# Two of four weight sums by accumulating DMA in the FFN, one pool of 4 KB tiles, and a deeper pipeline

## The chip, the cores and the metric

The kernel runs on one core of a Trainium2 chip, at batch 1 with 512 tokens. The engines that matter are TensorE (PE in the profile; its weight loads stand apart as PEld), VectorE (DVE), ScalarE (ACT), GpSimd (POOL) and SyncE (SP). DVE, ACT and POOL do elementwise work. SP and POOL also issue the DMAs: plain loads go through SP, and loads that add onto what already lies in the destination tile (accumulate DMAs) go through POOL. Each engine works through its instructions in a fixed order, and waits on semaphores for what others must have done first.

The metric is the device time of one execution in microseconds (us). Besides the time of each run there is one profiled execution with its trace.

## The reference, cut to what matters

```python
D_MODEL = 1024; SEQ = 512; DEPTH = 2; CHUNK = 128; RET_HEADS = 4; FFN_HIDDEN = 2816

def sgu_mixer(h, w_in, w_s, b_s, ln_g, ln_b, w_out):
    u, v = jnp.split(jax.nn.gelu(h @ w_in), 2, axis=-1)
    v = layernorm(v, ln_g, ln_b)                   # then in chunks of 128 tokens, 8 groups
    mixed = jnp.einsum('gts,bcsgd->bctgd', tril(w_s), v) + b_s
    return (u * mixed) @ w_out

def retention(h, positions, w_in, gn_g, w_out):
    q, k, v, g = split(h @ w_in)                   # 4 heads; q and k 256 wide, v and g 512 wide
    q, k = rotary(q, positions), rotary(k, positions) * 256 ** -0.5
    o = chunkwise_recurrence(q, k, v)              # decayed causal scores in chunks, state between
    o = rms(o) * gn_g
    return (o * jax.nn.silu(g)) @ w_out

def swiglu(h, w_gu, w_down):
    a, b = jnp.split(h @ w_gu, 2, axis=-1)         # each 2816 wide
    return (jax.nn.silu(a) * b) @ w_down

def reference(x, ...):
    h = x
    h = h + sgu_mixer(rmsnorm(h)); h = h + swiglu(rmsnorm(h))     # layer 0
    h = h + retention(rmsnorm(h)); h = h + swiglu(rmsnorm(h))     # layer 1
    return rmsnorm(h, final_norm_g)
```

All is float32.

## The kernel before, in words

**Precision.** Each operand of a large product is split into two halves of type float32r: ACT copies the high half (`wh`, L187) and DVE subtracts to get the low half (`wl`, L188). `three` then issues three matmuls for each product of tiles: high by high (L209), high by low (L210), low by high (L211).

**Seven products in place of eight.** Most large weight matrices go through `seven`, which multiplies two-by-two blocks with seven products, in the order P1, P7, P6, Q4, P5, P2, P3. Four of the seven need a sum of weight blocks: P7 (a tile `t`), P6 and Q4 (which add two more blocks to the same `t`), and P5 (`b12` with `b11`). The left factors, sums of blocks of the activations, come from `combos` (names with `h_P7h`, `z_P6l` and so on; `xA` does it for the FFN's input, `xP_f`). A product is cut into two groups of two 128-row tiles of weight; one group of one product is a *job*, so one call of `seven` has 14 jobs.

**Where the weight sums are made.** With `dma_sums=True` (the FFN's down projections `dn`, the retention's `vg` and `ro0`) the sums of P7 and P5 are made by the load itself: SP loads one block, then POOL issues an accumulate DMA of the other block onto the same tile (`onto`, L292), which must wait for the first. The sums of P6 and Q4 are made by DVE (`add`, L315). In the FFN's gate-and-up units, `gu`, all four sums are made by DVE.

**The FFN.** One FFN runs `gl` (the leftover 256 columns of each half), then units `gu_0`, `gu_1`, `dn_0`, `gu_2`, `gu_3`, `dn_1`, `gu_4`, then `dn_2`. The `gu` units are `turned`: their matmuls are 128x256, and 336 of them make one unit. A `dn` unit has 168 matmuls of 128x512 and adds into the residual `X`. `last_rows` does the rest of a layer's last product (`so`, `ro1`, `dn_2`), token chunk by token chunk, so that the next norm can begin early: the normed rows are transposed and split into `XH` (ACT, L591) and `XL` (DVE, L592), on which the next layer's first matmuls wait.

**Layer 0's mixer** projects `v0`, `v1`, `u0`, `u1`, normalizes `v` (L765), mixes over tokens (L794), and gates `u` (L782 to L785). **Layer 1's mixer** runs for each head `qk`, `vg`, the scores and the values; then `ro0` (a `seven`) and `ro1`.

**Rotary tables.** The sine and cosine for the retention are worked out on DVE (L825 to L862) in small steps that are put between the jobs of layer 0's FFN (`extra`, `more`).

**What sets the order.** `pipeline` walks over the jobs. Before job number `done` runs, the loads of all jobs below `done + FETCH` (6) have been issued, and the splits of all jobs below `done + PREP` (3):

```python
while f < len(weighted) and f < done + FETCH:
    jobs[weighted[f]].fetch()
...
while p < len(weighted) and p < done + PREP:
    jobs[weighted[p]].prep()
```

A scheduler places the instructions of each engine in an order that starts from this one. Weight tiles come from the pool `gen` of 21 tiles of 4 KB per partition; raw activations and left factors of `last_rows` come from `raws`, 8 tiles of 8 KB; `XH` and `XL` are one fixed buffer each.

Of the kernel before, what the change touches and what calls it, by code (L numbers as in the profile page):

```python
# [25 lines left out]
PREP = 3  # L26
FETCH = 6
N_GEN = 21
N_RAW = 8
N_TMP = 5  # L30
EPS = 1e-6
# [18 lines left out]
class Job:  # L50


    def __init__(self, fetch=None, prep=None, run=None):
        self.fetch, self.prep, self.run = fetch, prep, run


def pipeline(jobs):
    n = len(jobs)
    weighted = [i for i, j in enumerate(jobs) if j.prep is not None]
    f = p = 0  # L60
    done = 0
    for i, job in enumerate(jobs):
        while f < len(weighted) and f < done + FETCH:
            jobs[weighted[f]].fetch()
            f += 1
        while p < len(weighted) and p < done + PREP:
            jobs[weighted[p]].prep()
            p += 1
        if job.prep is not None:
            done += 1  # L70
        job.run()
# [3 lines left out]
def trunk(ctx, tc, x, positions, mix_g, ffn_g, fin_g, sgu_w_in, sgu_w_s, sgu_b_s, sgu_ln_g, sgu_ln_b,  # L75
# [5 lines left out]
    raws = ctx.enter_context(tc.tile_pool(name="raws", bufs=N_RAW))  # L81
# [10 lines left out]
    def RAW(name, dtype=F32, shape=(P, 4, T)):  # L92
        return raws.tile(list(shape), dtype, tag="r", name=name)
# [11 lines left out]

    def captured(*fns):

        n = len(jobs)
        for fn in fns:
            fn()  # L110
        new = jobs[n:]
        del jobs[n:]
        units = []
        for j in new:
            if j.prep is not None or not units:
                units.append([j])
            else:
                units[-1].append(j)
        return units

    def merged(a, b):

        i = j = 0
        while i < len(a) or j < len(b):
            if j == len(b) or (i < len(a) and i * len(b) <= j * len(a)):
                jobs.extend(a[i])
                i += 1
            else:
                jobs.extend(b[j])
                j += 1  # L130
# [143 lines left out]

    def seven(name, w, r0, np_, c1, c2, A, evac, mid=None, dma_sums=False, turned=False):

# [3 lines left out]
        steps = [(s, min(2, np_ - s)) for s in range(0, np_, 2)]  # L280
# [4 lines left out]
        def load(key, i, j, s, nk):  # L285
            raw[key, s] = fetch_tile(f"{name}_{key}_{s}", w, r0 + i * np_ + s, nk, ((c1, T) if j == 0 else (c2, T),))

        def onto(key, i, j, s, nk):
            c0 = c1 if j == 0 else c2
            k0 = r0 + i * np_ + s  # L290
            src = w[k0 * P:(k0 + nk) * P, c0:c0 + T].rearrange("(a p) n -> p a n", p=P)
            nc.gpsimd.dma_start(raw[key, s][:, 0:nk, :], src, accum_op=ALU.add)  # L292

        def fetch(p, s, nk):
            if p == "P1":
                load("b11", 0, 0, s, nk)
            elif p == "P7" and dma_sums:
                load("t", 1, 1, s, nk)
                onto("t", 0, 1, s, nk)
            elif p == "P5" and dma_sums:  # L300
                load("b12", 0, 1, s, nk)
                onto("b12", 0, 0, s, nk)
            elif p == "P7":
                load("b12", 0, 1, s, nk)
                load("t", 1, 1, s, nk)
            elif p == "Q4":
                load("b21", 1, 0, s, nk)
            elif p == "P2":
                load("b21", 1, 0, s, nk)
            elif p == "P3":  # L310
                load("b22", 1, 1, s, nk)

        def add(dst, other, s, nk):
            d, o = raw[dst, s][:, 0:nk, :], raw[other, s][:, 0:nk, :]
            nc.vector.tensor_tensor(d, d, o, ALU.add)  # L315

        def prep(p, s, nk):
            use = {"P1": "b11", "P7": "t", "P6": "t", "Q4": "t", "P5": "b12", "P2": "b21", "P3": "b22"}[p]
            extra = {"P7": "b12", "P6": "b11", "Q4": "b21", "P5": "b11"}.get(p)
            if extra and not (dma_sums and p in ("P7", "P5")):  # L320
                add(use, extra, s, nk)
            parts[p, s] = split(raw[use, s], f"{name}_{p}_{s}", nk)

        chain = {"P1": "X", "P7": "Y", "P6": "X", "Q4": "Y", "P5": "X", "P2": "Z", "P3": "X"}
# [802 lines left out]
```

## Time and profile before

| quantity | value |
|---|---|
| median of 3 runs | 1269.76 us (1268.45 to 1273.49) |
| profiled execution, its own time | 1267.79 us |
| span of its trace | 1266.1 us |
| instructions in the trace | 18063 |
| PE busy | 1220.4 us, 96% of the span |
| DVE busy | 947.4 us, 75% |
| ACT busy | 616.8 us, 49% |
| POOL busy | 47.4 us, 4% |
| DMA moved | 183.91 MB, mean 145 GB/s |

A row of the list of waits reads: engine, the line that waited, the instruction and line it waited for, then the microseconds in total, how often, and the longest. A row of windows gives a stretch of the trace, its length, the busy time of each engine in it, then the clock granted to PE as a share of full speed, the busy share of the 16 DMA engines and what they moved. In the timeline a row is one instruction with its start and its duration, and in brackets the idle time just before it. A matmul's duration reaches past the start of the next one, since matmuls are pipelined, so the distance between two starts is the cost of one. In the list of DMAs, SPq and POOLq are the queues of SP and POOL, and the last number is the median time from issue to landing.

### The profile page before, as it was taken

Reading aid. Unit: us, or ns where it says so; the run is one execution under the profiler, and the core shown is the slowest. Engines: PE = TensorE matmul, PEld = TensorE weight load, DVE = VectorE, ACT = ScalarE, POOL = GpSimd, SP = SyncE. Lnnn points to the kernel's source line nnn. Section 1 sums busy time; section 2 is a strip of 40 time slices with the busy share of each in tenths; the row PEclk is TensorE's granted clock in tenths of the full one; section 3 lists DMA queues with packets and bytes.
Section 4 is the critical chain, followed back from the end, with each engine's and each line's share of the span. In section 5 each row is a group of like instructions: output and inputs, shape, how many; then the busy total and the mean of one; then the engine's idle time right before and its main releaser. Section 6 shows DMA issues by size and latency. Waiting matters only on the chain. (4 is left out here: it accounts for less than half of the span.)

```text
span 1266.1 us, 18063 instructions
## 1 busy us (share of the span) xinstructions
PE 1220.4 (96%) x7290; PEld 1081.8 (85%) x7290; DVE 947.4 (75%) x1080; ACT 616.8 (49%) x772; POOL 47.4 (4%) x49
## 2 busy tenths in 40 slices
PE   8999999998999999999999999889999999999997
PEld 7787889987999798978878878668899989997995
DVE  4467489999779884786766757697488799878864
ACT  4424255544544463656455564465355445544452
POOL 0000000000001000000000000000000010000000
PEclk9999999999999999999999999899999999999999
DMA  7224225457636763356445645466215476556531
GB/s 266 85 83 128 64 84 156 137 146 228 183 117 164 219 198 94 84 156 169 127 140 125 185 123 150 110 178 211 84 44 174 142 175 196 170 158 187 189 116 67
DMA packets 101987, 183.91 MB, mean 145 GB/s; under 512 B 6376, under 2 KB 19728, under 8 KB 101904
## 3 DMA queue, kind: packets, MB, share of 16 engines
q1 hardware_dynamic: 91984, 163.86, 40.8%
q0 software_dynamic: 9920, 18.90, 9.1%
q8 instruction: 57, 0.93, 0.3%
q14 instruction: 26, 0.21, 0.1%
HBM read 180.64 MB, written 2.10 MB: 144 GB/s over the span
## 5 line engine op out<-in xcount | busy, mean ns | idle before, releaser
L211 PE MATMUL X_gu<-xP_f,wl_gu_P 128*128 128x256 f32 x480 | 135.8, 283 | 0.0
L210 PE MATMUL X_gu<-xP_f,wh_gu_P 128*128 128x256 f32 x480 | 135.8, 283 | 0.0
L209 PE MATMUL X_gu<-xP_f,wh_gu_P 128*128 128x256 f32 x480 | 135.8, 283 | 0.0
L188 DVE TENSOR_TENSOR wl_gu_P<-wr_gu_b,wh_gu_P 128x1024 fp32r<-128x1024 f32 x80 | 95.0, 1219 | 29.6 <-ACT wh_gu_P L187 29.6
L210 PEld LDWEIGHTS X_gu<-xP_f,wh_gu_P 128*128 128x128 f32 x480 | 92.1, 192 | 0.2
L209 PEld LDWEIGHTS X_gu<-xP_f,wh_gu_P 128*128 128x128 f32 x480 | 92.1, 192 | 0.2
L211 PEld LDWEIGHTS X_gu<-xP_f,wl_gu_P 128*128 128x128 f32 x480 | 92.1, 192 | 0.0
L187 ACT ACTIVATE wh_gu_P<-wr_gu_b 128x1024 fp32r<-128x1024 f32 x80 | 79.5, 1052 | 18.4 <-DVE wl_gu_P L188 5.0
L315 DVE TENSOR_TENSOR wr_gu_t<-wr_gu_t,wr_gu_b 128x1024 f32<-128x1024 f32 x60 | 71.7, 1217 | 2.1 <-DMA wr_gu_t<-in_ffn_w_gu 2.0
L187 ACT ACTIVATE wh_gu_P<-wr_gu_t 128x1024 fp32r<-128x1024 f32 x40 | 41.6, 1057 | 50.3 <-DVE wr_gu_t L315 40.6
L188 DVE TENSOR_TENSOR wl_vg_P<-wr_vg_b,wh_vg_P 128x1024 fp32r<-128x1024 f32 x32 | 38.6, 1219 | 26.8 <-ACT wh_vg_P L187 26.8
L209 PE MATMUL ps_qk<-XH,wh_qk 128*128 128x512 f32 (+1 forms) x160 | 56.1, 352 | 1.4 <-ACT xr_r L622 0.8
L211 PE MATMUL ps_qk<-XH,wl_qk 128*128 128x512 f32 (+1 forms) x160 | 55.6, 348 | 0.0
L210 PE MATMUL ps_qk<-XL,wh_qk 128*128 128x512 f32 (+1 forms) x160 | 55.4, 347 | 0.0
L188 DVE TENSOR_TENSOR wl_gu_P<-wr_gu_t,wh_gu_P 128x1024 fp32r<-128x1024 f32 x40 | 48.0, 1218 | 7.1 <-ACT wh_gu_P L187 7.1
L209 PE MATMUL Y_gu<-xP_f,wh_gu_P 128*128 128x256 f32 x160 | 45.3, 283 | 0.0
L210 PE MATMUL Y_gu<-xP_f,wh_gu_P 128*128 128x256 f32 x160 | 45.3, 283 | 0.0
L211 PE MATMUL Y_gu<-xP_f,wl_gu_P 128*128 128x256 f32 x160 | 45.3, 283 | 0.0
L209 PE MATMUL Y_gu<-XH,wh_gu_Q 128*128 128x256 f32 x160 | 45.3, 283 | 0.0
L210 PE MATMUL Y_gu<-XL,wh_gu_Q 128*128 128x256 f32 x160 | 45.3, 283 | 0.0
L211 PE MATMUL Y_gu<-XH,wl_gu_Q 128*128 128x256 f32 x160 | 45.3, 283 | 0.0
L209 PE MATMUL Z_gu<-XH,wh_gu_P 128*128 128x256 f32 x160 | 45.3, 283 | 0.0
(507 smaller groups left out, 3872.9 us busy)
## 6 DMA issues: line engine op xcount, KB each, us to landing
wr_gu_b<-in_ffn_w_gu SPq DMA_DIRECT2D x100, 512.0 KB, 4.0
wr_dn_b<-in_ffn_w_down SPq DMA_DIRECT2D x40, 512.0 KB, 4.6
wr_vg_b<-in_ret_w_in SPq DMA_DIRECT2D x40, 512.0 KB, 3.7
wr_gu_t<-in_ffn_w_gu SPq DMA_DIRECT2D x20, 512.0 KB, 5.2
wr_qk<-in_ret_w_in SPq DMA_DIRECT2D x32, 256.0 KB, 3.1
wr_dn<-in_ffn_w_down SPq DMA_DIRECT2D x12, 512.0 KB, 4.0
wr_ro_b<-in_ret_w_out SPq DMA_DIRECT2D x10, 512.0 KB, 4.1
wr_u<-in_sgu_w_in SPq DMA_DIRECT2D x8, 512.0 KB, 4.1
```

The source lines that it names most:

```text
L187: nc.scalar.activation(h, s, AF.Copy)
L188: nc.vector.tensor_tensor(l, s, f32(h), ALU.subtract)
L209: nc.tensor.matmul(o, ah, bh, start=start, stop=False, skip_group_check=True)
L210: nc.tensor.matmul(o, ah, bl, start=False, stop=False, skip_group_check=True)
L211: nc.tensor.matmul(o, al, bh, start=False, stop=stop, skip_group_check=True)
L315: nc.vector.tensor_tensor(d, d, o, ALU.add)
```

## The change

**Constants.** `PREP` goes from 3 to 5 and `FETCH` from 6 to 8. A job whose load is an accumulate (`early`) is fetched 12 jobs ahead (`EARLY`), past the jobs between.

**Pools.** `raws` goes away, and `gen` grows from 21 to 38 tiles of 4 KB. What was held in 8 KB tiles is now held in halves (`xr`, `hq`, `zq`, `yq`, the pairs of `xA`, the left factors of `last_rows`). `XH` and `XL` come from a pool of two buffers and are new tiles for every norm.

**Sums.** In the ten `gu` units the sums of P7 and P5 are made by accumulate DMAs too, as in `dn`, `vg` and `ro0`: four accumulates of 512 KB for each unit, forty in all, in place of forty additions on DVE. The number of plain loads of a unit stays at 12 of 512 KB, since `b12` is now loaded for P5 where it had been loaded for P7.

**Left factors.** P1, P7 and P6 of a `dn` unit are asked for during the last three products of the `gu` unit before it, those of `ro0` during the last head's `vg`, and those of `last_rows` during `ro0` and `gu_4`.

**Last product.** In `seven`, only the last two groups of P3 wait for each other; with two groups this is what was there before.

**Rotary tables.** Their steps move out of layer 0's FFN and stand between the jobs of `u0` and `u1` in layer 0's mixer (`turn_tables`).

```diff
-PREP = 3
-FETCH = 6
-N_GEN = 21
-N_RAW = 8
+PREP = 5
+FETCH = 8
+EARLY = 12
+ASK = 3
+N_GEN = 38
+SUMS_X = ("P7", "P5")
+SUMS_GU = ("P7", "P5")
...
 def pipeline(jobs):
...
+    for job in jobs:
+        while e < n and e < done + EARLY:
+            if weighted[e].early:
+                weighted[e].fetch()
+            e += 1
+        while f < n and f < done + FETCH:
+            if not weighted[f].early:
+                weighted[f].fetch()
             f += 1
+        while p < n and p < done + PREP:
+            weighted[p].prep()
             p += 1
...
-    raws = ctx.enter_context(tc.tile_pool(name="raws", bufs=N_RAW))
+    xp = ctx.enter_context(tc.tile_pool(name="xp", bufs=2))
...
+        def fetch(p, g, s, nk):
+            def load(key, i, j):
+                raw[key, g, s] = G(f"wr_{name}_{key}_{g}_{s}")
+                nc.sync.dma_start(raw[key, g, s][:, 0:nk, :], source(i, j, g, s, nk))
+
+            def onto(key, i, j):
+                nc.gpsimd.dma_start(raw[key, g, s][:, 0:nk, :], source(i, j, g, s, nk), accum_op=ALU.add)
+
+            if p == "P7":
+                load("t", 1, 1)
+                (onto if p in dma_sums else load)("t" if p in dma_sums else "o", 0, 1)
+            elif p == "P1":
+                load("b11", 0, 0)
+            elif p == "Q4":
+                load("b21", 1, 0)
+            elif p == "P2":
+                load("b21", 1, 0)
+            elif p == "P5":
+                load("b12", 0, 1)
+                (onto if p in dma_sums else load)("b12" if p in dma_sums else "o", 0, 0)
...
+            jobs.append(Job(lambda p=p, st_=st_: fetch(p, *st_), lambda p=p, st_=st_: prep(p, *st_), lambda i=i: run(i),
+                            early=p in dma_sums))
...
-    project_t("u0", w_in, ((0, T),), after_u0, mix0_col)
-    project_t("u1", w_in, ((T, T),), after_u1, mix0_col)
+    project_t("u0", w_in, ((0, T),), after_u0, mix0_col, mid={kp: turn_tables for kp in range(4)})
+    project_t("u1", w_in, ((T, T),), after_u1, mix0_col, mid={kp: turn_tables for kp in range(4)})
...
-            seven(f"gu{l}_{i}", w, 0, 4, i * T, FF + i * T, xparts, evac, mid, turned=True)
+            seven(f"gu{l}_{u}", w, rows(0, KD), u * T, FF + u * T, xparts, evac, mid, dma_sums=SUMS_GU, turned=True)
...
-        unit(1, {"P5": lambda: A[0]("P1"), "P2": lambda: A[0]("P7")})
+        unit(1, {("Q4", 1): lambda: A[0]("P1", 0), ("P5", 0): lambda: A[0]("P7", 0), ("P2", 1): lambda: A[0]("P6", 0)})
         down(0)
...
-        second({"P2": lambda: outA("P1")} if hd == 3 else None)
+        second({("P6", 1): lambda: outA("P1", 0), ("P2", 0): lambda: outA("P7", 0), ("P2", 1): lambda: outA("P6", 0)} if hd == 3 else None)
```

Three places of the new order are needed later on. A row is the line, the kind of instruction and the names of what it writes and reads, with the shape.

**DVE where layer 0's FFN begins.** `XL` is the low half of the normed input, for which `gl`'s matmuls wait; `wl_gu_0_P` are the low halves of `gu_0`'s first weights; L315 are weight sums. Before:

```order
L603 SCALAR_TENSOR_TENSOR xs_f_0_1302<-X,nf_so_1295,g_f_1145 128x1024
L188 TENSOR_TENSOR wl_gl_3_1335<-wr_gl_3_1099,wh_gl_3_1334 128x1024
L592 TENSOR_TENSOR XL<-xT_f_1_1338,XH 128x8x128
L188 TENSOR_TENSOR wl_gu_0_P_0_1380<-wr_gu_0_b_0_1112,wh_gu_0_P_0_1379 128x1024
L315 TENSOR_TENSOR wr_gu_0_t_1332<-wr_gu_0_t_1332,wr_gu_0_b_0_1330 128x1024
L188 TENSOR_TENSOR wl_gu_0_P_2_1408<-wr_gu_0_b_2_1124,wh_gu_0_P_2_1407 128x1024
L315 TENSOR_TENSOR wr_gu_0_b_0_1330<-wr_gu_0_b_0_1330,wr_gu_0_b_0_1112 128x1024
L315 TENSOR_TENSOR wr_gu_0_t_1377<-wr_gu_0_t_1377,wr_gu_0_b_2_1375 128x1024
L188 TENSOR_TENSOR wl_gu_0_P_0_1450<-wr_gu_0_t_1332,wh_gu_0_P_0_1449 128x1024
L656 TENSOR_TENSOR xS_f_1477<-xr_f_0_1213,xr_f_1_1214 128x1024
L592 TENSOR_TENSOR XL<-xT_f_0_1411,XH 128x8x128
```

Now:

```order
L595 SCALAR_TENSOR_TENSOR xs_f_0_1414<-X,nf_so_1407,g_f_1255 128x1024
L170 TENSOR_TENSOR wl_gu_0_P_0_2_1446<-wr_gu_0_b_0_2_1214,wh_gu_0_P_0_2_1445 128x1024
L584 TENSOR_TENSOR XL_f_1322<-xT_f_1_1449,XH_f_1321 128x8x128
L170 TENSOR_TENSOR wl_gu_0_P_0_0_1492<-wr_gu_0_t_0_1144,wh_gu_0_P_0_0_1491 128x1024
L584 TENSOR_TENSOR XL_f_1322<-xT_f_0_1525,XH_f_1321 128x8x128
L302 TENSOR_TENSOR wr_gu_0_t_0_1144<-wr_gu_0_t_0_1144,wr_gu_0_b_0_0_1202 128x1024
```

Between the last two `XL` there stood seven instructions, three of them weight sums; now there stands one.

**SP where the FFN goes from `gu_3` to `dn_1` (layer 0).** Rows are loads of weight tiles. `t` and `b12` of `dn_1` are the tiles onto which POOL then accumulates. Before:

```order
L179 DMA wr_gu0_3_b21_0_3423<-in_ffn_w_gu 128x2x512
L179 DMA wr_gu0_3_b21_2_3464<-in_ffn_w_gu 128x2x512
L179 DMA wr_gu0_3_b22_0_3495<-in_ffn_w_gu 128x2x512
L179 DMA wr_gu0_3_b22_2_3528<-in_ffn_w_gu 128x2x512
L179 DMA wr_dn0_1_b11_0_3558<-in_ffn_w_down 128x2x512
L179 DMA wr_dn0_1_b11_2_3594<-in_ffn_w_down 128x2x512
L179 DMA wr_dn0_1_t_0_3625<-in_ffn_w_down 128x2x512
L179 DMA wr_dn0_1_t_2_3664<-in_ffn_w_down 128x2x512
```

Now:

```order
L277 DMA wr_gu0_3_b21_0_0_3409<-in_ffn_w_gu 128x2x512
L277 DMA wr_gu0_3_b21_0_2_3444<-in_ffn_w_gu 128x2x512
L277 DMA wr_dn0_1_t_0_0_3474<-in_ffn_w_down 128x2x512
L277 DMA wr_gu0_3_b22_0_0_3477<-in_ffn_w_gu 128x2x512
L277 DMA wr_dn0_1_t_0_2_3509<-in_ffn_w_down 128x2x512
L277 DMA wr_gu0_3_b22_0_2_3512<-in_ffn_w_gu 128x2x512
L277 DMA wr_dn0_1_b11_0_0_3542<-in_ffn_w_down 128x2x512
L277 DMA wr_dn0_1_b11_0_2_3578<-in_ffn_w_down 128x2x512
```

`t` of `dn_1` moved from behind `dn_1`'s own first loads to ahead of `gu_3`'s last.

**DVE in layer 0's mixer, ahead of the normalization of `v`.** `turns`, `turn`, `frac` and `sum` are the rotary tables' steps; `ry_ln` is the end of the chain for the variance; `v_0` and `v_1` are what is normalized. Before:

```order
L526 SCALAR_TENSOR_TENSOR ru_ln_564<-rt_ln_562,ra_ln 128x4
L528 SCALAR_TENSOR_TENSOR ry_ln_566<-ru_ln_564,ry_ln_560 128x4
L765 TENSOR_SCALAR v_0_324<-v_0_324,mv,ry_ln_566 128x512 x2
L765 TENSOR_SCALAR v_0_329<-v_0_329,mv,ry_ln_566 128x512 x2
L765 TENSOR_SCALAR v_1_529<-v_1_529,mv,ry_ln_566 128x512 x2
```

Now:

```order
L735 TENSOR_TENSOR frac_763<-turns_761,turn_764 128x512
L518 SCALAR_TENSOR_TENSOR ry_ln_576<-ru_ln_574,ry_ln_570 128x4
L757 TENSOR_TENSOR sum_767<-turns,frac_763 128x512
L514 TENSOR_TENSOR rt_ln_578<-ry_ln_576 128x4
L734 CAST turn_769<-sum_767 128x512
L516 SCALAR_TENSOR_TENSOR ru_ln_580<-rt_ln_578,ra_ln 128x4
L735 TENSOR_TENSOR turns<-sum_767,turn_769 128x512
L518 SCALAR_TENSOR_TENSOR ry_ln_582<-ru_ln_580,ry_ln_576 128x4
L811 TENSOR_SCALAR v_0_324<-v_0_324,mv,ry_ln_582 128x512 x2
```

The steps of the tables now alternate with the chain of `ry_ln`; eighteen of them, from the one that writes `ahl` on, stand ahead of the normalization, where there was none.

503 lines of the change are left out of this document (231 added, 272 removed).

## The prediction

> **What bounds the kernel now.** I read the page first, then the waits of PE, then windows of 30 us to see where those waits lie, then the timeline at the longest.
>
> ```profile
> span 1266.1 us, 18063 instructions
> PE 1220.4 (96%) x7290; PEld 1081.8 (85%) x7290; DVE 947.4 (75%) x1080; ACT 616.8 (49%) x772; POOL 47.4 (4%) x49
> q1 hardware_dynamic: 91984, 163.86, 40.8%
> q0 software_dynamic: 9920, 18.90, 9.1%
> ```
>
> PE is the bound, with 45.7 us of its span idle. The change does not take matmuls away, so its gain can only come from PE's idle time and from time in which PE ran at a lower clock. The longest waits:
>
> ```profile
> PE ps_gl L210 <- DVE XL L592: 5.2, 4, 2.5
> PE X_ro L209 <- ACT wh_ro_P L187: 4.4, 2, 2.7
> PE X_dn L209 <- ACT wh_dn_P L187: 3.5, 3, 1.7
> PE Y_dn L209 <- ACT wh_dn_Q L187: 3.2, 4, 2.6
> PE Z_vg L210 <- DVE wl_vg_P L188: 2.0, 3, 1.0
> PE X_vg L210 <- DVE wl_vg_P L188: 1.8, 1, 1.8
> PE X_ro L210 <- DVE wl_ro_P L188: 1.7, 2, 0.9
> PE pv L209 <- ACT vh L1012: 1.6, 2, 0.8
> PE Y_ro L209 <- ACT wh_ro_Q L187: 1.1, 1, 1.1
> PE Y_dn L209 <- ACT wh_dn_P L187: 1.1, 1, 1.1
> ```
>
> They add up to 25.6 us in 23 waits. No row is of a `gu` unit: they are of `gl`, `dn`, `vg` and `ro0`. The windows agree (the columns are the stretch, its length, PE, PEld, DVE, ACT, POOL, clock, DMA share, GB/s):
>
> ```profile
> 0.00:30.00 30.00, 25.55 (x111) 21.32 (x112) 15.42 (x33) 13.65 (x20) 3.14 (x12) 1.00 0.81 281
> 210.00:240.00 30.00, 30.00 (x253) 30.00 (x251) 29.58 (x34) 14.29 (x15) 0.00 (x0) 1.00 0.49 150
> 270.00:300.00 30.00, 26.82 (x122) 21.94 (x121) 27.71 (x27) 12.99 (x14) 3.25 (x3) 0.94 0.73 192
> 390.00:420.00 30.00, 28.07 (x146) 23.38 (x146) 27.83 (x26) 12.29 (x12) 2.92 (x3) 1.00 0.74 176
> 780.00:810.00 30.00, 25.96 (x114) 20.68 (x113) 19.99 (x23) 15.57 (x18) 2.41 (x3) 0.93 0.62 150
> 810.00:840.00 30.00, 27.27 (x110) 21.20 (x110) 22.35 (x32) 15.14 (x28) 2.42 (x2) 0.95 0.39 109
> 840.00:870.00 30.00, 27.77 (x123) 22.31 (x122) 28.42 (x30) 22.27 (x28) 0.00 (x0) 0.94 0.77 233
> ```
>
> In a `gu` window (210) PE is full although DVE is busy for 29.58 us of 30; a DVE addition there costs PE nothing. In the `dn` windows (270, 390) and in `ro0` (780 to 870) PE waits, and in 270 and the three of `ro0` the granted clock is lower as well.
>
> **Why the weights come late.** The jobs of `seven` are short. 253 matmuls of 128x256 in 30 us make 0.119 us each, so a `gu` unit of 336 lasts 40 us and one of its 14 jobs 2.9 us; a `dn` job, 12 matmuls of 128x512 at 0.227 us (by the starts below), 2.7 us. Loads of a job are asked 6 jobs ahead and its split 3 ahead: three jobs, 8 to 9 us, lie between. An accumulated tile takes two loads after each other:
>
> ```profile
> wr_dn_t<-in_ffn_w_down SPq DMA_DIRECT2D x8, 512.0 KB, 3.8
> wr_dn_t<-in_ffn_w_down POOLq DMA_DIRECT2D x8, 512.0 KB, 6.1
> wr_dn_b<-in_ffn_w_down POOLq DMA_DIRECT2D x8, 512.0 KB, 8.5
> ```
>
> That is 3.8 + 6.1 to 8.5 us, with about 1.2 us of POOL to issue (2.42 for two, window 810): 11 to 14 us, which is 2 to 5 us more than the gap between asking and splitting. The split, which has three jobs' time itself, then starts late behind ACT's and DVE's other rows, and PE waits for `wh_dn` and `wl_dn`.
>
> **The change part by part.**
>
> *More look-ahead for accumulated tiles (12 ahead, split 5 ahead).* Seven jobs, 19 to 20 us, now lie between, against the same 11 to 14: 5 to 9 us are left over, and splits stand two jobs (5 to 6 us) further ahead of their matmuls. On SP the early `t` stands ahead of two plain loads (front, second place); one such load is 0.524 MB, 1.7 us at the 317 GB/s worked out below, so a plain load may land up to 3.3 us later than now. Plain loads keep three jobs between asking and splitting (8 and 5), and the split's own lead of five jobs, 14 us, takes that up: cost nothing, and 3 us once for each `dn` (12 in all) if SP stands still for a free tile. The waits of `dn` above (3.5, 3.2, 1.1) are 7.8; I let 7.0 go. Of `vg` (2.0, 1.8) and `pv` (1.6), 5.4, I let 3.5 go, since `pv` waits for a split of values, not of weights. At worst none of the 13.2 goes, at best all.
>
> *Left factors earlier.* Of `ro0`'s 4.4, 1.7 and 1.1 (7.2) I let 4.5 go: the weights come in time, but `z_P6l`, the sums, and residual additions crowd DVE there as before. Bounds 0 and 7.2. The same sums now stand in the `gu` unit ahead, whose window 210 shows PE full with DVE at 29.58; if that cover were gone, six rows of 1.22 us for each `dn` would be the loss, 7 us.
>
> *Additions off DVE.* Forty of these go:
>
> ```profile
> L315 DVE TENSOR_TENSOR wr_gu_t<-wr_gu_t,wr_gu_b 128x1024 f32<-128x1024 f32 x60 | 71.7, 1217 | 2.1 <-DMA wr_gu_t<-in_ffn_w_gu 2.0
> ```
>
> 40 x 1.217 = 48.7 us of DVE, 4% of the span. Inside `gu` this is worth nothing: PE is full there. It counts where the FFN begins, in the wait for `XL`:
>
> ```profile
> 170.99 1.22 DVE L315 TENSOR_TENSOR wr_gu_t<-wr_gu_t,wr_gu_b 128x1024 f32<-128x1024 f32 x1
> 173.26 1.22 DVE L315 TENSOR_TENSOR wr_gu_b<-wr_gu_b,wr_gu_b 128x1024 f32<-128x1024 f32 x1
> 174.39 1.22 DVE L315 TENSOR_TENSOR wr_gu_t<-wr_gu_t,wr_gu_b 128x1024 f32<-128x1024 f32 x1
> 177.80 1.22 DVE L592 TENSOR_TENSOR XL<-xT_f,XH 128x1024 fp32r<-128x1024 f32 x1
> ```
>
> Three sums of 1.22 stand ahead of the last `XL`, 3.7 us for a wait whose longest is 2.5; in the new order (front, first place) they are gone. Of 5.2 I let 4.2 go (bounds 0 and 5.2).
>
> *Clock and the hidden part of a stall.* Starts of PE's matmuls around the longest wait of `dn_0` in the timeline, and shortly after:
>
> ```profile
> 285.46 0.39 PE L211 MATMUL X_dn<-wh_dn_P,h_P6l 128*128 128x512 f32 x1
> 285.69 0.39 PE L209 MATMUL X_dn<-wh_dn_P,h_P6h 128*128 128x512 f32 x1
> 288.68 0.47 PE L209 MATMUL Y_dn<-wh_dn_Q,h_Q4h 128*128 128x512 f32 x1 [2.61 <-ACT wh_dn_Q L187]
> ...
> 291.25 0.63 PE L209 MATMUL X_dn<-wh_dn_P,h_P6h 128*128 128x512 f32 x1
> 291.68 0.63 PE L210 MATMUL X_dn<-wl_dn_P,h_P6h 128*128 128x512 f32 x1
> ```
>
> A start comes 0.23 us after the one before; over the stall it is 2.99, so the stall costs 2.76 where 2.61 is shown, 0.15 more. Of the 23 waits about 19 should go or shrink to nothing: 19 x 0.15 = 2.9. Two microseconds after that stall the distance is 0.43: half the clock. By the clock column, windows 270, 780, 810 and 840 lost (0.06 + 0.07 + 0.05 + 0.06) x 30 = 7.2 us of full-speed time. They are the windows with the longest waits; I let 5.5 go (bounds 0 and 7.2), keeping some for what stays at `ro0`.
>
> The Trainium skill ("TensorE: Matmul & The Clock Gate", Why this matters for your kernels) has the clock fall back only after PE idles for more than about 3 us between bursts. Here it fell after a gap shown as 2.61, so the row decides; if the page's threshold held, these falls would have another cause and the sum would be 5.5 smaller (the last but one rival).
>
> *Forty more accumulates.* Bytes by time give 163.86 MB / (0.408 x 1266.1) = 317 GB/s at full share for plain loads, and 18.90 / (0.091 x 1266.1) = 164 for accumulates. A `gu` unit will have 12 x 0.524 = 6.3 MB plain (19.8 us) and 2.1 MB accumulated (12.8): 32.6 of its 40 us, a share of 0.81, where window 210 shows 0.49. That share is the one of window 0 and little over 0.74 to 0.77 of windows 390 and 840, so I expect it to be carried. New waits for accumulated `gu` tiles: lead 20 against 11 to 14, so at best 0; at worst it is a rival below. I take 1 us. POOL will issue 28 accumulates in one FFN, 34 us of about 317; it has no other work there, but issues in order, so one accumulate that waits for its plain load holds those behind it.
>
> *Rotary tables.* Eighteen steps stand ahead of the normalization of `v`:
>
> ```profile
> L847 DVE TENSOR_SCALAR turns<-ahl x6: 417/418/420, 195.0 to 248.1; 128x512 f32<-128x512 f32 x6
> L840 DVE TENSOR_TENSOR frac<-turns,turn x5: 681/682/694, 198.7 to 252.7; 128x512 f32<-128x512 f32 x5
> ...
> 71.21 3.74 DVE L765 TENSOR_SCALAR v<-v,mv,ry_ln 128x512 f32<-128x512 f32 x8
> ...
> 85.48 1.95 PE L794 MATMUL mix<-wst,v 128*128 128x128 f32 x16
> ```
>
> Eight with one input at 0.42 and ten with two at 0.68: 10.2 us. The normalization ended at 74.95 and the matmuls that need it began at 85.48, 10.5 us later, so the steps alone just fit; splits that PREP 5 puts ahead (two or so, 1.2 us each) do not. Cost 0 to 2.6; I take 1.5. The FFN's DVE loses the same work, which is worth nothing there, since PE is full.
>
> *Tiles and buffers.* Halves in place of 8 KB tiles add a few rows to ACT and DVE where those have time (DVE at 75%); new buffers for `XH` and `XL` take away a wait that the list does not show. Both cost nothing; if 30 rows of 0.2 us lay on the path, 6.
>
> *Sum.* 7.0 + 3.5 + 4.5 + 4.2 + 2.9 + 5.5 = 27.6 gained, 1.0 + 1.5 lost: 25 us, against the profiled execution's own 1267.79 us. The median of the runs, 1269.76, stands 2.0 above it; so 1269.8 - 25 gives 1244, or 1243 with a little of the waits under 1 us that are not in the list above. A measurement of this kernel can tell about 0.5%, 6.3 us, from no change.
>
> **Rivals.**
>
> *The stalls only move (still faster).* At `XL`, in `ro0` and with `dn`'s residual additions DVE and ACT themselves are the late ones: window 840 has DVE busy for 28.42. Then only the accumulate waits go: 7.0 + 2.0 of `vg` and some clock, 3, less 2.5 lost: about 10 us, 1260. For it: `XL` and `X_ro` wait for engines with a full row. Against it: DVE loses 48.7 us.
>
> *DMA becomes the bound (slower).* One FFN's weights are 5 x 8.4 + 2 x 8.4 + 5.2 = 64 MB. It takes 317 us now (five `gu` units of 40, two `dn` of 38, `gl` and `dn_2`), so it needs 202 GB/s throughout, a quarter of it accumulated. The most seen with accumulates is 176 and 192 (windows 390, 270). If 190 were the ceiling, an FFN lasts 64 / 190 = 337 us, 20 more; two of them 40, less 27 gained on the way, plus 1.5: about 1283. It decides at 202 GB/s. Against it: those windows had a share of 0.73, so the engines idled a quarter of the time.
>
> *Accumulates land later with the load (no change).* If both loads took 1.5 times as long at a share of 0.81, 18.5 + 1.2 would use up the 20 us of lead; at 1.65 times they are 1.5 us late at each of the 20 sums of P7 and P5, 30 us for both FFNs, and the gain is gone: 1270.
>
> *The clock stays low (faster, by less).* The falls come in windows where DMA, DVE and PE change pace together, so they could belong to the place and not to the gap. Then 5.5 of the sum stay: 1248.5. Against it: 291 us, where the distance doubles, follows 2 us behind the longest gap of its window.
>
> *More goes (faster still).* All the bounds at their best: 13.2 + 7.2 + 5.2 + 7.2 + 3.4 = 36, 1234; with the shorter waits too, 1228.
>
> **How the numbers follow.** The forecast gets 0.45, the clock that stays low 0.06, the stalls that move 0.20, DMA as the bound 0.12, late accumulates 0.09, more 0.08. The predicted time is that of the forecast, 1243. From 1228 to 1267 lie nearly all of the forecast and of the clock's rival, the moved stalls, most of the best case and the milder late accumulates: 0.8. Faster: 0.45 + 0.06 + 0.17 + 0.08 = 0.76; the same: 0.03 of the moved stalls and 0.06 of late accumulates, 0.09; slower: 0.12 and the other 0.03, 0.15.
>
> **What would show it.** Right: no wait of PE for `wh_dn` over 1 us; waits for the last `XL` under 1 us; a DMA share near 0.8 in `gu` windows with PE full; the clock at 1.00 in windows of `dn`; DVE's busy time near 900 us. Wrong: PE waiting in `gu` for `wh_gu_P` whose releaser is an accumulate; a share over 0.9 with less than 200 GB/s; more than 3 us of waits at `u0` or `u1` for `v`.

## The result and the profile after

The changed kernel takes 1232.8 us (median of 4 runs, 1232.24 to 1234.5), against 1269.92 before. The ratio is 0.9706, with a 95% interval of 0.9684 to 0.9728: 37 us faster, where 27 were forecast with the time of 1243. The profiled execution took 1232.99 us; its span is 34.9 us shorter than before.

The page of the changed kernel:

```profile
span 1231.2 us, 18104 instructions
PE 1208.1 (98%) x7290; PEld 1078.7 (88%) x7290; DVE 902.0 (73%) x1052; ACT 606.0 (49%) x772; POOL 95.4 (8%) x89
q1 hardware_dynamic: 91984, 163.86, 40.3%
q0 software_dynamic: 20800, 39.87, 19.1%
```

PE's idle time went from 45.7 to 1231.2 - 1208.1 = 23.1 us, 22.6 less. PE's busy time went down by 12.3 us with the same 7290 matmuls. About 7 of it is the lower clock: 7.2 by the rounded clock column of the prediction, 6.8 by the clock records in the trace before, which have 13.7 us at half clock ahead of the last 40 us, where the changed kernel has none. The rest, 5 us, is a remainder and no row measures it; the part of each stall that lies under the recorded duration of a matmul is the likely place. What PE still waits for:

```profile
PE mix_ps L150 <- DMA mix_rows<-in_mix_norm_g: 3.1, 1, 3.1
PE Y_dn L193 <- DVE h_Q4l L397: 2.5, 4, 0.6
PE ps_v L191 <- ACT wh_v L173: 2.0, 1, 2.0
PE ps_gl L192 <- DVE XL_f L584: 1.7, 4, 0.6
PE Y_ro L191 <- ACT wh_ro_P L169: 1.6, 1, 1.6
...
PE ps_u L191 <- DVE add_b L801: 0.6, 1, 0.6
```

No wait for `wh_dn` or `wl_vg` is left; of `ro0` one of 1.6 us is. The windows at the places that the prediction named (`gu_0`, `dn_0`, the `gu` unit after it, `dn_1`, the start of `ro0`):

```profile
180.00:210.00 30.00, 30.00 (x252) 30.00 (x252) 22.61 (x21) 16.86 (x17) 2.38 (x2) 1.00 0.63 175
270.00:300.00 30.00, 29.36 (x140) 24.27 (x139) 28.61 (x27) 15.31 (x16) 2.39 (x2) 1.00 0.80 218
300.00:330.00 30.00, 30.00 (x216) 28.42 (x216) 22.10 (x20) 14.52 (x15) 4.79 (x4) 1.00 0.96 269
390.00:420.00 30.00, 29.37 (x140) 24.25 (x139) 28.60 (x27) 15.29 (x16) 2.38 (x2) 1.00 0.80 220
780.00:810.00 30.00, 28.41 (x129) 23.27 (x128) 28.13 (x33) 20.77 (x28) 2.41 (x2) 1.00 0.61 170
```

The clock is 1.00 in all of them. DMA carries 269 GB/s at a share of 0.96 and PE is full beside it.

### The profile page after: what moved, and what is told of

It is laid out like the page before. It is cut to its first block, busy times and chain, and to the rows that moved or that the text cites. A ratio compares the mean times of both kernels' runs of the same rounds, so it can differ in the third digit from the quotient of the medians.

```text
span 1231.2 us, 18104 instructions
## 1 busy us (share of the span) xinstructions
PE 1208.1 (98%) x7290; PEld 1078.7 (88%) x7290; DVE 902.0 (73%) x1052; ACT 606.0 (49%) x772; POOL 95.4 (8%) x89
## 3 DMA queue, kind: packets, MB, share of 16 engines
q1 hardware_dynamic: 91984, 163.86, 40.3%
q0 software_dynamic: 20800, 39.87, 19.1%
## 4 chain that ended last, share of the span: by engine, by line
PE 87%; DVE 8%; ACT 3%; issue 2%; DMA 0%; SPq 0%; DVEq 0%; ACTq 0%
PE X_gu L192 6%; PE X_gu L193 6%; PE X_gu L191 6%; PE Y_gu L193 3%; PE Y_gu L192 3%; PE Y_gu L191 3%; PE X_vg L191 2%; PE X_vg L193 2%; PE X_vg L192 2%; PE ps_qk L192 2%; PE ps_qk L193 2%; PE ps_qk L191 2%; PE X_dn L191 2%; PE X_dn L192 2%; PE X_dn L193 2%; PE ps_dn L191 2%
## 5 line engine op out<-in xcount | busy, mean ns | idle before, releaser
L169 ACT ACTIVATE wh_gu_P<-wr_gu_b 128x1024 fp32r<-128x1024 f32 x80 | 80.3, 1050 | 19.3 <-DMA wr_gu_b<-in_ffn_w_gu 15.4
L192 PE MATMUL ps_qk<-XL_r,wh_qk 128*128 128x512 f32 (+1 forms) x160 | 55.7, 348 | 0.6 <-DVE XL_r L584 0.6
L191 PE MATMUL ps_qk<-XH_r,wh_qk 128*128 128x512 f32 (+1 forms) x160 | 55.5, 349 | 0.0
L193 PE MATMUL ps_qk<-XH_r,wl_qk 128*128 128x512 f32 (+1 forms) x160 | 55.2, 348 | 0.0
L302 DVE TENSOR_TENSOR wr_gu_t<-wr_gu_t,wr_gu_b 128x1024 f32<-128x1024 f32 x40 | 47.6, 1218 | 0.1
L191 PE MATMUL Y_gu<-xP7h_f,wh_gu_P 128*128 128x256 f32 x160 | 45.3, 283 | 0.0
L192 PE MATMUL Y_gu<-xP7l_f,wh_gu_P 128*128 128x256 f32 x160 | 45.3, 283 | 0.0
L193 PE MATMUL Y_gu<-xP7h_f,wl_gu_P 128*128 128x256 f32 x160 | 45.3, 283 | 0.0
L191 PE MATMUL X_gu<-xP6h_f,wh_gu_P 128*128 128x256 f32 x160 | 45.3, 283 | 0.0
L192 PE MATMUL X_gu<-xP6l_f,wh_gu_P 128*128 128x256 f32 x160 | 45.3, 283 | 0.0
L193 PE MATMUL X_gu<-xP6h_f,wl_gu_P 128*128 128x256 f32 x160 | 45.3, 283 | 0.0
L191 PE MATMUL Y_gu<-XH_f,wh_gu_Q 128*128 128x256 f32 x160 | 45.3, 283 | 0.0
```

Of the source, the lines that this page charges most:

```text
L169: nc.scalar.activation(h, s, AF.Copy)
L191: nc.tensor.matmul(o, ah, bh, start=start, stop=False, skip_group_check=True)
L192: nc.tensor.matmul(o, ah, bl, start=False, stop=False, skip_group_check=True)
L193: nc.tensor.matmul(o, al, bh, start=False, stop=stop, skip_group_check=True)
```

## The experiments

All kernels are timed against the kernel before on the same chip, whose median was 1272.3 to 1272.6 in these comparisons, some 2 us above the first one. Differences between two changed kernels of under 3 us are therefore not read from medians alone. Each median is of four runs, those of e_prep3 and e_late_prep3 of ten.

| kernel | median us | ratio to before | 95% interval |
|---|---|---|---|
| changed kernel | 1232.8 | 0.9706 | 0.9684 to 0.9728 |
| e_dve_sums: gu sums on DVE | 1233.2 | 0.9697 | 0.9671 to 0.9724 |
| e_load2: idle loads added | 1232.6 | 0.9669 | 0.9653 to 0.9684 |
| e_rot_back: rotary back in the FFN | 1239.5 | 0.9739 | 0.9725 to 0.9754 |
| e_no_early: accumulates not asked early | 1245.8 | 0.9796 | 0.9764 to 0.9827 |
| e_best: left factors earlier still | 1246.6 | 0.9789 | 0.9763 to 0.9814 |
| e_late_left: left factors late | 1253.9 | 0.9857 | 0.9823 to 0.9892 |
| e_no_acc: no accumulates | 1266.2 | 0.9950 | 0.9935 to 0.9965 |
| e_late_prep3: left factors late, splits 3 ahead | 1271.2 | 0.9988 | 0.9975 to 1.0001 |
| e_prep3: splits 3 ahead | 1277.3 | 1.0037 | 1.0020 to 1.0053 |
| e_old_dve: old look-ahead, gu sums on DVE | 1290.2 | 1.0124 | 1.0104 to 1.0145 |
| e_old_look: old look-ahead | 1292.1 | 1.0149 | 1.0112 to 1.0187 |
| e_look_only: before, with look-ahead raised | 1292.3 | 1.0136 | 1.0118 to 1.0154 |

**Is it the look-ahead?** The theory on record: accumulated tiles landed after their splits were due, so look-ahead is the gain. The rival: DVE had too much to do.

```diff
-PREP = 5
-FETCH = 8
-EARLY = 12
+PREP = 3
+FETCH = 6
+EARLY = 6
```

> The changed kernel with the look-ahead of before (loads 6 jobs ahead, accumulated ones too, splits 3 ahead); sums by DMA, pool, left factors and rotary tables as changed. Late accumulates are the cause: waits of PE for wh_dn, wl_dn and wl_vg come back, 7 + 3.5 us, with some of the lower clock, 3 to 4: about 1246 (13 above the changed kernel's 1232.8), and now the gu units have such waits too, up to 10 more. DVE's load is the cause: under 3 us slower, since its 40 additions stay away.

1292.1: the loss is 59 us, not 13, nor 23 with the most allowed for `gu`. The rival of DVE's load falls, but the theory's size is far off. By the trace PE is idle for 57.6 us, 34.5 more than in the changed kernel, where 10.5 were expected, and 47.8 us at half clock cost 24 more, where 3 to 4 were. The same without the forty accumulates:

```diff
-SUMS_GU = ("P7", "P5")
+SUMS_GU = ()
```

> The changed kernel with the look-ahead of before (6, 6, 3) and the gu sums of P7 and P5 on DVE: what is left of the change is the pool, the left factors, the rotary tables. Sums in gu have been seen to be worth nothing by themselves (1233.2 with them on DVE). If look-ahead is what the change lives on: 15 to 25 slower than 1232.8, so 1248 to 1258, with waits for wh_dn, wl_vg, wh_ro in PE's list. If the forty accumulates alone made the old look-ahead bad (1292): 1235 to 1240.

1290.2, far above both cases, so the accumulates are not what hurts; what is left of the change without its look-ahead is slower than the kernel before by 1.2%. And the other way round, the two constants raised in the kernel before:

```diff
-PREP = 3
-FETCH = 6
+PREP = 5
+FETCH = 8
```

> The kernel before with its two constants alone raised (loads 8 jobs ahead, splits 5). Look-ahead alone is what counts: 1245 to 1255. The pool of 21 tiles holds it back: loads wait longer for a free tile, no gain or a loss, 1265 to 1290; I take the second to be likelier, since each split two jobs further ahead holds four more tiles of 21.

1292.3, just above the upper end of the second case. Neither the look-ahead alone (in the pool of 21 tiles) nor the rest alone is faster than before; together they give 37 us. PE's longest waits moved to work that is not weights, here `xs_f` and the left factors:

```profile
PE xT_f L589 <- DVE xs_f L603: 8.0, 4, 2.1
PE X_dn L211 <- DVE h_P6l L415: 5.7, 3, 1.9
```

That loads wait longer for free tiles was the reason given, and the trace does not bear it out: the waits of SP's weight loads (L179) add up to 1072 us against 1048 before, and of PE's rows of over 1 us only `wh_qk` with 2.8 us is for weights, beside the 2.0 for `wh_v` that every list here has. Which part of the order of DVE and ACT holds PE there was not worked out.

**Which part of the look-ahead?** First the early accumulates alone, splits still 5 ahead:

```diff
-EARLY = 12
+EARLY = 8
```

> The changed kernel with accumulated loads asked 8 jobs ahead like the others, not 12; splits stay 5 ahead. Three jobs (8 to 9 us) then lie between asking and splitting, against 11 to 14 us for the two loads. Late accumulates are the cause and the splits' lead of 5 jobs does not cover it: 6 to 10 us slower, 1239 to 1243. The splits' lead covers it: within 2 us, 1233 to 1235. DVE's load is the cause: no change.

1245.8, 13 us slower, above the upper end of the first case; the profiled run was the fastest of the four, 1242.98, 10 us slower. The new waits are not at `dn` but where a `gu` unit follows `dn`, at the first of the new accumulated tiles. On ACT:

```profile
1031.17 1.06 ACT L169 ACTIVATE wh_gu_P<-wr_gu_t 128x1024 fp32r<-128x1024 f32 x1 [7.70 <-DMA wr_gu_t<-in_ffn_w_gu]
```

and on PE:

```profile
PE Y_gu L191 <- ACT wh_gu_P L169: 4.4, 2, 3.2
```

So the early loads are needed for the forty accumulates that the same change adds. Then the splits alone, with as many jobs between asking and splitting as in the changed kernel (loads and splits both stand two jobs nearer to their matmuls):

```diff
-PREP = 5
-FETCH = 8
-EARLY = 12
+PREP = 3
+FETCH = 6
+EARLY = 10
```

> The changed kernel with splits 3 ahead, plain loads 6 and accumulated ones 10: the same jobs between asking and splitting as in the changed kernel (3 and 7), but the split's own lead as before. If only late loads count: within 3 us of 1232.8. If the split's lead over ACT's and DVE's queues counts: 6 to 15 slower, with PE waiting for wl_dn, wl_ro and wl_vg though the loads have landed.

1277.3, 44 us slower than the changed kernel, with the loads as far ahead of the splits as there; the case that came true had 6 to 15. In the trace 27.4 us are more idle time of PE and 15.4 come from 30.7 us at half clock. The waits are back at `dn`:

```profile
PE X_dn L191 <- ACT wh_dn_P L169: 13.4, 4, 3.4
PE X_vg L192 <- DVE wl_vg_P L170: 4.8, 6, 2.1
PE X_ro L191 <- ACT wh_ro_P L169: 3.9, 1, 3.9
```

ACT's timeline ahead of `dn_1` says why. `s` (L904) is the SiLU of the `gu` unit, which waits for PE; `h_P6h` is a left factor; `wh_dn_P` from `wr_dn_b` is `dn`'s first weight:

```profile
392.87 1.06 ACT L904 ACTIVATE s<-s 128x1024 f32<-128x1024 f32 x1 [7.47 <-DVE s L903]
394.06 1.06 ACT L396 ACTIVATE h_P6h<-h_S 128x1024 fp32r<-128x1024 f32 x1
395.03 1.99 ACT L169 ACTIVATE wh_dn_P<-wr_dn_b 128x1024 fp32r<-128x1024 f32 x2
```

ACT stood idle for 7.47 us with the splits of two landed tiles behind the SiLU in its order: the loads of P1's weights had landed at 381.04 and 382.36. In the changed kernel, ahead of `dn_0`, the same split stands ahead of the same SiLU:

```profile
258.00 1.99 ACT L169 ACTIVATE wh_dn_P<-wr_dn_b 128x1024 fp32r<-128x1024 f32 x2
266.38 1.06 ACT L904 ACTIVATE s<-s 128x1024 f32<-128x1024 f32 x1 [6.39 <-DVE s L903]
267.57 1.06 ACT L396 ACTIVATE h_P6h<-h_S 128x1024 fp32r<-128x1024 f32 x1
268.54 1.99 ACT L169 ACTIVATE wh_dn_P<-wr_dn_t 128x1024 fp32r<-128x1024 f32 x2
```

ACT waits nearly as long there, 6.39 us, but with P1's weights done. So the depth of PREP decides on which side of an instruction that waits for PE a split falls. This is shown for `dn`; the waits at `vg` and `ro0` were not followed in the same way.

**Left factors.** Their early requests taken back (an excerpt; the last head's and the last rows' likewise):

```diff
-        unit(1, {("Q4", 1): lambda: A[0]("P1", 0), ("P5", 0): lambda: A[0]("P7", 0), ("P2", 1): lambda: A[0]("P6", 0)})
+        unit(1, {("P5", 1): lambda: A[0]("P1", 0), ("P2", 1): lambda: A[0]("P7", 0)})
...
-    seven("ro0", ret_w_out[0], rows(0, 8), 0, T, outA, into_x, {("P7", 1): heads[3][3], ("P2", 1): heads[3][2], ("P5", 0): lambda: lefts["ro1"](0, 1), ("P5", 1): lambda: lefts["ro1"](0, 0)}, SUMS_X)
+    seven("ro0", ret_w_out[0], rows(0, 8), 0, T, outA, into_x, {("P7", 1): heads[3][3], ("P2", 1): heads[3][2]}, SUMS_X)
```

> The changed kernel with the left factors asked as late as before (of dn's P1 and P7 in the unit ahead, P6 in dn; of ro0 only P1 ahead; of the last rows when used). My theory: ro0's waits come back, 4.5 us, and 2 to 3 us of lower clock, and 1 to 2 us at dn: 7 to 9 us slower, 1240 to 1242. Only the weights were late: within 2 us of 1232.8.

1253.9, 21 us slower, where 7 to 9 were expected, and not at `ro0`:

```profile
PE X_dn L193 <- DVE h_P6l L397: 8.0, 4, 2.0
PE ps_ro L191 <- ACT ro_h L445: 5.4, 1, 5.4
```

P6's left factor of `dn` costs 2.0 us in each of the four units, the left factors of `ro1` 5.4 once. By the trace 12.1 us of the loss are more idle time of PE, and 8.5 come from 17.1 us at half clock that follow these waits.

Two edits, each made or not, give four kernels. The fourth has this edit and that of e_prep3 together:

> The changed kernel with late left factors and the short look-ahead together (splits 3 ahead, loads 6 and 10), the fourth corner beside 1232.8 (neither), 1253.9 (late left factors) and 1277.3 (short look-ahead). If the two cost PE the same places independently, 1277.3 + 21 = 1298. If early left factors hurt only because they stand ahead of late splits on ACT and DVE, taking them back helps: 1262 to 1272, near the kernel before.

1271.2: the second case, at its upper end. With splits 3 ahead, early left factors make it slower (1277.3 against 1271.2); with splits 5 ahead they make it faster by 21 us (1232.8 against 1253.9). The two parts need each other; that they share ACT's and DVE's orders is the likely reason.

**Sums off DVE.** In `gu` first:

```diff
-SUMS_GU = ("P7", "P5")
+SUMS_GU = ()
```

> The changed kernel with the sums of P7 and P5 in the gu units by DVE again (both blocks loaded plainly, 16 loads to a unit). My theory: the additions lie beside a full PE in gu and count only for XL where the FFN begins, 2 x 2 us: 4 us slower, 1237. DVE's load is the cause of most of the gain: 15 or more slower, 1248. DVE busy time 902 + 48.7 = 951 us in both.

1233.2: nothing. DVE is busy for 44.8 us more and PE no less:

```profile
PE 1208.6 (98%) x7290; PEld 1079.3 (88%) x7290; DVE 946.8 (77%) x1092; ACT 608.8 (49%) x772; POOL 47.4 (4%) x49
```

Not even the wait for `XL` is longer, it is 1.7 us in 4 as in the changed kernel. With the additions back on DVE none of them stands ahead of the last `XL` (L302 is a weight sum):

```profile
174.67 1.23 DVE L170 TENSOR_TENSOR wl_gu_P<-wr_gu_t,wh_gu_P 128x1024 fp32r<-128x1024 f32 x1 [2.10 <-ACT wh_gu_P L169]
175.81 1.22 DVE L584 TENSOR_TENSOR XL_f<-xT_f,XH_f 128x1024 fp32r<-128x1024 f32 x1
176.94 1.22 DVE L302 TENSOR_TENSOR wr_gu_t<-wr_gu_t,wr_gu_b 128x1024 f32<-128x1024 f32 x1
```

Then everywhere, with this besides:

```diff
-SUMS_X = ("P7", "P5")
+SUMS_X = ()
```

> The changed kernel with no accumulate DMA at all: all weight sums, of dn, vg and ro0 too, by DVE, plain loads in their place. If DMA sums are worth their DVE time where DVE is full (28.6 of 30 us in the dn windows): 36 x 1.22 = 44 us of DVE, of which I expect 5 to 12 on the path, 1238 to 1245. If look-ahead hides DVE there as it does in gu: within 2 us of 1232.8.

1266.2, 33 us slower than the changed kernel and far above both cases, for 36 additions more than in the kernel just shown. They are not slow, they stand in the wrong place, in `dn`, where DVE had 28.6 of 30 us:

```profile
PE Y_dn L192 <- DVE wl_dn_P L170: 13.4, 4, 3.4
PE Y_vg L191 <- ACT y L995: 4.2, 4, 1.2
...
PE Y_ro L191 <- ACT wh_ro_P L169: 2.9, 1, 2.9
```

and the clock is lower there:

```profile
270.00:300.00 30.00, 26.64 (x122) 22.02 (x121) 27.34 (x26) 17.01 (x17) 0.00 (x0) 0.94 0.65 209
```

DVE's timeline in `dn_0` shows the place. With two sums ahead of them, the low halves of both of P7's tiles come behind the residual addition (`X`, L410), which waits for PE; in the changed kernel the first of them starts at 269.81, ahead of the same addition at 272.37:

```profile
272.70 1.22 DVE L410 TENSOR_TENSOR X<-X,X_dn 128x1024 f32<-128x1024 f32 x1 [2.62 <-PE X_dn L193]
273.84 1.22 DVE L397 TENSOR_TENSOR h_P6l<-h_S,h_P6h 128x1024 fp32r<-128x1024 f32 x1
274.97 2.35 DVE L170 TENSOR_TENSOR wl_dn_P<-wr_dn_t,wh_dn_P 128x1024 fp32r<-128x1024 f32 x2
```

PE's wait there is 3.36 us. This kernel also holds one more tile for each of these sums; what that alone costs was not separated.

**DMA as the bound.** Four loads that nothing reads, in each `gu` unit:

```diff
                 load("b22", 1, 1)
+            if turned and p in ("P6", "Q4"):
+                load("idle", 1, 0)
```

> The changed kernel with four idle loads of 0.524 MB more in each gu unit (nothing reads them): 10.5 MB in 40 us, a queue share near 0.98 by 317 and 164 GB/s. By those rates PE is still fed: under 6 us slower, up to 1239. If the ceiling were 190 to 202 GB/s, a gu unit would take 52 us and the kernel 1350.

1232.6: nothing again, with 20.97 MB more. Two of its windows:

```profile
210.00:240.00 30.00, 30.00 (x252) 30.00 (x251) 22.71 (x21) 11.98 (x12) 2.40 (x2) 1.00 0.81 243
300.00:330.00 30.00, 30.00 (x218) 28.50 (x217) 22.10 (x20) 14.90 (x16) 4.79 (x4) 1.00 1.07 327
```

327 GB/s with accumulates among them, and PE full. The share can read a little over 1, so 0.96 is not to be taken for the last 4% of room. The rival that set the ceiling at 190 is refuted.

**Rotary tables.** Their steps back in the FFN, as before after `gl` and after P6 and P5 of each unit of layer 0:

```diff
-    project_t("u0", w_in, ((0, T),), after_u0, mix0_col, mid={kp: turn_tables for kp in range(4)})
-    project_t("u1", w_in, ((T, T),), after_u1, mix0_col, mid={kp: turn_tables for kp in range(4)})
+    project_t("u0", w_in, ((0, T),), after_u0, mix0_col)
+    project_t("u1", w_in, ((T, T),), after_u1, mix0_col)
...
                     copy("u2", acc["X"])
+                    more()
...
-    feed_forward(0, normed("r", mix_g[1:2], raw_copy("r")))
+    feed_forward(0, normed("r", mix_g[1:2], raw_copy("r")), turn_tables)
```

> The changed kernel with the rotary steps back between the jobs of layer 0's FFN. The forecast put their new place at 0 to 2.6 us of cost, 1.5 taken: back in the FFN they should give 0 to 1.5 us, 1231 to 1233. If DVE's row in the FFN is what had to be cleared: 3 to 6 slower, 1236 to 1239.

1239.5: 6.7 us slower by median, 7.0 by span (1238.2 against 1231.2), 4 by the ratios to before, whose intervals just touch the changed kernel's. One new wait makes most of it, in `dn_0` only, with a fall of the clock at it, worth 1.7 us:

```profile
PE Y_dn L192 <- DVE wl_dn_P L170: 2.8, 1, 2.8
```

```profile
270.00:300.00 30.00, 26.92 (x123) 22.08 (x122) 28.02 (x27) 17.98 (x18) 3.61 (x3) 0.94 0.74 210
```

The last steps reach into `dn_0` (so they did in the kernel before, where the last one started at 273.48), ahead of that split on DVE:

```profile
268.61 0.69 DVE L735 TENSOR_TENSOR quarter_turns<-quarter,turn 128x512 f32<-128x512 f32 x1
```

As in e_no_acc, both low halves of P7 then come behind the residual addition, which waits 1.93 us for PE. Another fall of the clock in this trace, at 40 us, also worth 1.7 us, lies in the mixer behind a wait that every trace has, so it is no effect of this edit (see the last section).

**A version meant to beat both.** Q4's left factor of `dn` asked in P3 of the unit ahead, and `ro0`'s three asked in P7 and P6 of the last head's `vg`:

```diff
-        unit(1, {("Q4", 1): lambda: A[0]("P1", 0), ("P5", 0): lambda: A[0]("P7", 0), ("P2", 1): lambda: A[0]("P6", 0)})
+        unit(1, {("Q4", 1): lambda: A[0]("P1", 0), ("P5", 0): lambda: A[0]("P7", 0), ("P2", 1): lambda: A[0]("P6", 0), ("P3", 0): lambda: A[0]("Q4", 0)})
...
-        second({("P6", 1): lambda: outA("P1", 0), ("P2", 0): lambda: outA("P7", 0), ("P2", 1): lambda: outA("P6", 0)} if hd == 3 else None)
+        second({("P7", 0): lambda: outA("P1", 0), ("P6", 0): lambda: outA("P7", 0), ("P6", 1): lambda: outA("P6", 0)} if hd == 3 else None)
```

> The changed kernel with two left factors earlier: Q4's of dn asked in P3 of the unit ahead, and P1, P7 and P6 of ro0 asked in P7 and P6 of the last head's vg. The waits left in the changed kernel are Y_dn for h_Q4l, 2.5 us in 4, and Y_ro for wh_ro_P behind z_P6h on ACT, 1.6. If both go without a new wait: 4 to 5 us faster, 1228.

1246.6, 14 us slower than the changed kernel, and the four runs spread from 1240.7 to 1248.0. The two waits did go, and another came in their place, in all four `dn` units:

```profile
PE X_dn L191 <- ACT wh_dn_P L169: 7.1, 4, 1.8
PE Z_vg L192 <- DVE wl_vg_P L170: 2.7, 1, 2.7
```

On ACT `h_Q4h` now stands between the two splits of P7, which are needed first:

```profile
268.35 1.04 ACT L169 ACTIVATE wh_dn_P<-wr_dn_t 128x1024 fp32r<-128x1024 f32 x1
269.30 1.05 ACT L396 ACTIVATE h_Q4h<-h 128x1024 fp32r<-128x1024 f32 x1
270.25 1.05 ACT L169 ACTIVATE wh_dn_P<-wr_dn_t 128x1024 fp32r<-128x1024 f32 x1
```

Idle time of PE is only 5.4 us of the loss in the profiled run. 10.2 come from the clock, which falls at each of these five waits, 20.5 us at half clock in all. The run of 1240.7 had a mean granted clock of 0.998 against 0.990 in the profiled one, so much of the spread is the clock.

## Why the prediction was right, and where its steps were not

**What bounds the kernel: right.** The gain came from PE's idle time and its clock: 22.6 us idle and about 7 of clock, with a remainder of 5 that the step on the hidden part of a stall would put under the matmuls, make the 34.9 us of the span. All three were under-sized: 19.2 of waits, 5.5 and 2.9 were let go. The quoted waits alone came out close, 7.8 of `dn` fell to 2.5, 5.4 of `vg` and `pv` to nothing, 7.2 of `ro0` to 1.6 and 5.2 at `XL` to 1.7, 19.8 us in all. The shorter waits outside that list gave some 3 us and were counted with 1.

**More look-ahead for accumulated tiles: right in its effect, wrong in its cause.** The step compared the time of two loads, 11 to 14 us, with three jobs, and took the split to be late because the tile was. In the kernel before, accumulated tiles were late for ACT, as in the first row here, but PE's longest wait of `dn`, 2.61 us, was for the second:

```profile
392.39 1.06 ACT L187 ACTIVATE wh_dn_P<-wr_dn_t 128x1024 fp32r<-128x1024 f32 x1 [2.71 <-DMA wr_dn_t<-in_ffn_w_down]
...
287.50 1.06 ACT L187 ACTIVATE wh_dn_Q<-wr_dn_t 128x1024 fp32r<-128x1024 f32 x1 [2.34 <-DVE wr_dn_t L315]
```

`wh_dn_Q` is of Q4, whose sum DVE makes from a plain load; that load had landed at 279.29, and the sum stood behind other rows on DVE, which was never idle, until 286.19. So the 3.2 us of `Y_dn` were read as those of a late accumulate and were not. With the loads early and the splits 3 ahead (e_prep3) the waits of `dn` are still there, 13.4 us. What counts is the place of a split in ACT's order, ahead of a SiLU that waits for PE. That 7.0 us were let go and 5.3 went is luck as far as the reason goes. Early loads matter too, 13 us, but for the accumulates in `gu` that the change itself brings. Whether early loads are worth anything without those was not tried.

**Left factors earlier: right sign, wrong place and size.** 4.5 us at `ro0` were let go, and nothing at `dn`. `ro0`'s quoted waits fell by 5.6, but with late left factors they stay away. Late requests cost 21 us, with 8.0 of waits for P6's left factor in `dn`, 5.4 at `ro1`, and 8.5 by the clock. The bound on the loss, 7 us for each `dn` without cover, was not needed.

**Additions off DVE: wrong.** The claim that they are worth nothing inside `gu` holds. The 4.2 us at `XL` were put down to three additions ahead of it, which the accumulates would take away. With the additions back on DVE the wait is the same 1.7, since they no longer stand ahead of it. What moved them was another part of the change. The wait is 1.6 or 1.7 in every kernel built on the changed one, with the short look-ahead, with late left factors and with the rotary steps back too; what these share is the pools and the order that comes with them, a part that the prediction put at nothing. It was not run by itself.

**Rotary tables: wrong sign.** Their new place was costed at 1.5 us. The list has one wait of 0.6 at the `u` projections for it, `add_b`, which is not in the list of e_rot_back. Leaving the FFN was costed at nothing, since PE is full in `gu`; but the last steps lay in `dn_0`, where DVE has no room, and clearing it gave 4 to 7 us, the upper figure with the 1.7 at 40 us in it. The cover was named for the wrong unit.

**Forty more accumulates, and DMA as the bound: the forecast right, the rival wrong.** The share forecast for `gu`, 0.81, came as 0.63 in window 180 and 0.96 in window 300; why the loads gather there was not traced. 317 and 164 GB/s held up as prices: the changed kernel's page gives 163.86 MB / (0.403 x 1231.2) = 330 and, for accumulates, 170. Reading the highest rate seen as a ceiling had nothing to carry it.

**Stalls only move: right for e_best, wrong for this change.** **Clock that stays low: wrong**; it is 1.00 in every window of the changed kernel up to the tail.

## What to carry to other kernels

Look-ahead is not only a matter of when data lands: the depth at which work is asked decides on which side of a blocked instruction it stands in each engine's order, and 44 us hung on that here while the loads were as far ahead of the splits as in the changed kernel (17 us with late left factors, 1271.2 against 1253.9). A cost of DVE time has to be priced where it falls: the same addition was worth nothing in `gu` and about 0.9 us each (33 us for 36, the lower clock included) in `dn`, `vg` and `ro0`. Parts of such a change cannot be added up: look-ahead alone, in the old pool, and the rest alone were each over 1% slower than before, and the two together 2.9% faster. Look-ahead with the larger pool and nothing else was not run.

## What the runs showed of the hardware

PE's clock fell after shorter gaps than the 2.6 us that the prediction read it from: in window 270 of e_best, with one wait of 1.8 us, the granted clock was 0.94, while the wait of 1.6 in window 780 of the changed kernel left it at 1.00.

```profile
270.00:300.00 30.00, 28.21 (x129) 23.38 (x128) 26.61 (x25) 15.25 (x16) 2.39 (x2) 0.94 0.76 218
```

The step from 1.00 to 0.94 over 30 us is 1.8 us of full-speed time, as much as the wait itself. But the length of a gap is not all that decides. The wait of 1.97 us for `wh_v` near 39 us is in all fourteen traces, and the clock falls behind it in three of them. One gap of 2.01 us (e_late_left, `dn_0`) left the clock alone and the next (`dn_1`) did not.

The clock records of the traces show what else decides. Ahead of the last 40 us each fall is to half clock and lasts 3.41 us or a whole multiple of it, and within one trace the falls start a whole number of 3.41 us apart. So time is cut into stretches of 3.41 us, and a fall comes at the end of one. Where a gap lies in these stretches can differ from run to run, which would explain the clocks of e_best's four runs, 0.990 to 0.998. The stretch with most of the first gap of e_late_left, the stretch with all of the second, and the one after that:

```profile
282.32:285.73 3.41, 1.88 (x8) 1.58 (x9) 3.41 (x4) 1.57 (x2) 0.00 (x0) 1.00 0.80 250
401.80:405.21 3.41, 1.47 (x8) 0.76 (x6) 2.94 (x4) 3.41 (x4) 0.00 (x0) 1.00 1.02 257
405.21:408.62 3.41, 3.34 (x8) 2.67 (x9) 3.41 (x5) 0.11 (x1) 0.00 (x0) 0.50 0.55 192
```

The first gap began ahead of its stretch, so that PE was idle for 1.53 us of 3.41, 45%, and the clock stayed; the second lay within one, 1.94 us or 57%, and the clock halved. From 45 us on and up to the last 40 us, the stretch ahead of each of the 53 falls in all traces had PE idle for 47% or more (52% or more in all but two), and no stretch at full clock without a fall behind it had more than 52%, by matmul ends that the profile models. So about half a stretch, 1.7 us, is the limit here: the changed kernel has no wait of that length between 45 us and its tail, and its clock stays at 1.00 there. The Trainium skill ("TensorE: Matmul & The Clock Gate", Why this matters for your kernels) puts the threshold at about 3 us; the rows here have falls after 1.8 and 2.0.

Accumulate DMAs kept their price under load: 164 GB/s at full share before, 39.87 MB / (0.191 x 1231.2) = 170 after, with twice as many.
